# Five pairs of up products in seven half-sized products instead of three, with one load for two of their steps, and the low parts of unaltered weights formed by a DMA

## The chip, the cores and the metric

The kernel runs on one core of one Trainium2 chip. The metric is the device time of one execution in microseconds (us); lower is better. The engines are named as in the profile: PE (matrix products; its weight loads are PEld), DVE (vector), ACT (scalar functions), POOL, and SP, which here only issues DMAs.

## The reference

One decoder layer on a sequence of 512 tokens with 1024 features: forgetting attention, a layer norm, a gated MLP with a causal convolution of width 3, a second layer norm, and a gated embedding at the end. The change touches only the MLP:

```python
def conv_ffn(x, w_up, conv_w, conv_b, w_down):
    u, g = jnp.split(x @ w_up, [FFN_DIM], axis=-1)      # 1024 -> 2 x 2816
    g = causal_dwconv(g, conv_w, conv_b)
    return (jax.nn.gelu(g, approximate=False) * u) @ w_down
```

All inputs and outputs are float32.

## The kernel before

**Products.** PE takes operands in a shorter float format (`F32R`). Each operand is cut into a high part and a low part (what the high part leaves), and a product is three matmuls: high by high, high by low, low by high (`three`, L137). The activations are cut once; the weights are cut as they stream in.

**The stream of weights.** The class `Weights` (L57) holds one list of units of at most 128 x 1024 elements (512 KB) in the order of use. A unit is loaded by SP into a `raw` buffer (`load_to`, L74; four buffers of the tag `raw`, and every fifth unit of the MLP goes into a fifth place that `W.more` names, L259). It is then cut (`cut_to`, L95): ACT copies the raw weights into `whi`, which rounds them (L113), and DVE subtracts `whi` from them into `wlo` (L119). There are five `whi` and five `wlo` buffers (`SPLIT_BUFS`). Where a unit has a `make` function, DVE first forms sums or differences of weight blocks, one unit ahead of the cut. `get(i, 4)` (L125) cuts up to unit i+4 before PE's work on unit i is written down, so the cut of unit i+4 can begin when PE has finished unit i-1. There is a third way to make a low part, `by_dma` (L114): ACT writes minus the high part, and POOL issues a DMA that adds the weights to it from memory. No unit of this kernel asks for it.

**The MLP.** The 2816 hidden features are 22 blocks of 128, numbered f, and eleven pairs of blocks, numbered j. Parts 0 to 2 of the loop (L794) have three pairs each, part 3 has two. A *plain* pair is four up products (gate and up for two blocks) of 24 matmuls with 512 columns each. A *halved* pair (`UP_PAIRS`: 4, 7 and 9) takes the 2 x 2 blocks of x by weights in seven half-sized products instead of eight, in four steps, each for the gate (s=0) and for the up half (s=1), in `up_step` (L681):

- step 0 uses unaltered weights of block f0 (two products of 12 matmuls with 256 columns). Then ACT copies one half of the bank aside and zeroes it there (L706, L707), and DVE adds the two halves into the tile E (L709);
- step 1 uses t1 and t2, differences of weight blocks that `t12` (L188) forms with two DVE subtractions from the raw unit and a 256 KB side load;
- step 2 uses a third difference, `t3` (L202), formed from a second load of the same weights; DVE adds the result to E (L718);
- step 3 uses a fourth, `t4` (L208), with one product.

After the last step of a halved pair come its two convolutions and products (`conv_product`, L724) and then `operands` (L733), which makes the sums and the high and low parts that the down product wants. A plain pair has its first block's convolution and product in between, and so only the second block's product and `operands` at its end.

The down product of part p is also a seven-product form (`down`, L749). It runs in twelve steps of part p+1, in the calls of `between`: three steps of unaltered weights (`ua`), three `ub` (t12), three `uc` (t3) and three `ud` (t4). After the last step of each kind, `give` (L773) has DVE add finished banks to y (L555, L557), two adds of 512 columns for each; the banks x, y and z of the next kind are opened only then. Each pair of parts 1 and 2 has four down steps between its own: pair 3 has `ua` x3 and `ub`, pair 4 has `ub` x2 and `uc` x2, pair 5 has `uc` and `ud` x3, and pairs 6, 7 and 8 the same again.

**Order.** From block 2 on, DVE and ACT run in the order of the text (`manual_schedule`, L806). PE, SP and POOL are ordered by the tile framework's planner. A halved pair holds its two banks (one for gate, one for up) from step 0 to step 3.

Of the kernel before, what the change touches and what calls it, by code (L numbers as in the profile page):

```python
# [9 lines left out]
F32 = mybir.dt.float32  # L10
# [6 lines left out]
P = 128  # L17
# [7 lines left out]
KD = D // P  # L25
# [5 lines left out]

CHUNKS = (None, (1,) * 12, (1,) * 12, (2, 1) * 4)

UP_PAIRS = (4, 7, 9)
HALF = S // 2
ALPHA = 2.0 ** 0.25
EPS = 1e-5
# [2 lines left out]
UNIT = 1024  # L40
# [5 lines left out]
RAW_BUFS = 4  # L46
# [10 lines left out]
class Weights:  # L57
# [3 lines left out]
    def __init__(self, tc, pool):  # L61
        self.tc, self.nc, self.pool = tc, tc.nc, pool
        self.units, self.raw, self.parts = [], {}, {}
        self.loaded = self.cut = 0
        self.more, self.pieces = {}, {}

    def add(self, src, n=UNIT, inner=None, make=None, home=None, by_dma=False):

# [2 lines left out]
        self.units.append((src, n, inner, make, home, by_dma))  # L71
        return len(self.units) - 1

    def load_to(self, i):  # L74
        while self.loaded < min(i, len(self.units)):
            src, n, inner, make, _, _ = self.units[self.loaded]
            if self.loaded in self.more:
                t = self.more[self.loaded]()
            else:
                t = self.pool.tile([P, UNIT], F32, tag="raw", name=f"raw{self.loaded}", bufs=RAW_BUFS)  # L80
            v = t[:, :n]
            if inner is not None:
                v = v.rearrange("p (a b) -> p a b", b=inner)
            self.nc.sync.dma_start(v, src)
            if make is not None:
                make(None)
            self.raw[self.loaded] = t
            self.loaded += 1

    def make(self, i):  # L90
        if i < len(self.units) and i not in self.pieces and self.units[i][3] is not None:
            self.load_to(i + 1)
            self.pieces[i] = self.units[i][3](self.raw[i])

    def cut_to(self, i):  # L95
        while self.cut < min(i, len(self.units)):
            self.load_to(self.cut + 1)

            self.make(self.cut)
            self.make(self.cut + 1)  # L100
            src, n, inner, make, home, by_dma = self.units[self.cut]
            t = self.raw.pop(self.cut)
            behind = ExitStack()
            if home is not None:
                hi, lo, first = home()
                behind.enter_context(self.tc.issue_after(first))
            else:
                hi, lo = [self.pool.tile([P, UNIT], F32R, tag=g, name=f"{g}{self.cut}", bufs=SPLIT_BUFS)
                          for g in ("whi", "wlo")]
            c = 0  # L110
            for piece in [t[:, :n]] if make is None else self.pieces.pop(self.cut):
                e = c + piece.shape[-1]
                self.nc.scalar.activation(hi[:, c:e], piece, AF.Copy)  # L113
                if by_dma:  # L114
                    self.nc.scalar.activation(lo[:, c:e], piece, AF.Copy, scale=-1.0)
                    self.nc.gpsimd.dma_start(lo[:, c:e].rearrange("p (a b) -> p a b", b=inner), src,
                                             accum_op=ALU.add)
                else:
                    self.nc.vector.tensor_sub(lo[:, c:e], piece, hi[:, c:e].bitcast(F32))  # L119
                c = e  # L120
            behind.close()
            self.parts[self.cut] = (hi, lo)
            self.cut += 1

    def get(self, i, ahead=1):  # L125
        self.cut_to(i + 1 + ahead)
        more = any(u in self.more for u in range(self.cut, self.cut + RAW_BUFS))
        self.load_to(self.cut + RAW_BUFS - (not more))
        return self.parts[i]


# [1 line left out]
def trunk_layer(ctx: ExitStack, tc: tile.TileContext, xT, x2d, pT, wqk, wv0, wv1, wv2, bf, wo, wup, cwb,  # L133
                wdn, wpl, wg, bg, gm, bm, gf, bff, out):
    nc = tc.nc
# [18 lines left out]
    def half_rows(w, k0, n, cols):  # L154
        return w[k0 * P:(k0 + n) * P, cols * 512:(cols + 1) * 512].rearrange("(k p) c -> p k c", p=P)

    W = Weights(tc, base)
# [23 lines left out]
    aside = []  # L181

    def side(i):


        return aside[0][:, i, :]

    def t12(b11, i):  # L188
        def make(t):
            if t is None:  # L190
                to = side(i)
                if len(b11.shape) == 3:
                    to = to.rearrange("p (a b) -> p a b", b=P)
                nc.sync.dma_start(to, b11)
                return None
            t1, t2 = t[:, :512], side(i)
            nc.vector.tensor_sub(t1, t1, t2)
            nc.vector.tensor_sub(t2, t[:, 512:], t1)
            return [t1, t2]
        return make  # L200
# [7 lines left out]
    def t4(i):  # L208
        def make(t):
            if t is None:  # L210
                return None
            nc.vector.tensor_sub(t[:, :512], t[:, :512], side(i))
            return [t[:, :512]]
        return make

    def down_units(part):
        def b_rows(j, k0, n, cols):
            return half_rows(wdn, 2 * j + k0, n, cols)

        js = PAIRS[part]  # L220
        return [(b_rows(j, 0, 2, 0), UNIT, None) for j in js] + \
            [(b_rows(j, 0, 2, 1), UNIT, t12(wdn[2 * j * P:(2 * j + 1) * P, 0:512], i))
             for i, j in enumerate(js)] + \
            [(b_rows(j, 0, 2, 1), UNIT, t3) for j in js] + \
            [(b_rows(j, 1, 1, 0), 512, t4(i)) for i, j in enumerate(js)]

    def up_units(j):

        f0, f1 = 2 * j, 2 * j + 1

        def unit(f, q, make=None, k0=0):
            return W.add(wup[f, 1 - q][:, k0:], n=(KD - k0) * P, inner=P, make=make)

        return (lambda q: unit(f0, q), lambda q: unit(f1, q, t12(wup[f0, 1 - q][:, :4], 3 + q)),
                lambda q: unit(f1, q, t3), lambda q: unit(f0, q, t4(3 + q), 4))

    u_up, u_dn = {}, [[] for _ in PAIRS]
    for part in range(4):
        fs = range(6 * part, min(6 * part + 6, NF))
        todo = down_units(part - 1) if part else []  # L240

        for i in range(2 * len(fs)):
            f, q = fs[i // 2], i % 2
            j, n = f // 2, i % 4
            if j in UP_PAIRS:
                stages = up_units(j)
                for st, sq in (((0, 0),), ((0, 1),), ((1, 0), (1, 1)), ((2, 0), (2, 1)))[n]:
                    u_up[j, st, sq] = stages[st](sq)
            else:
                u_up[f, q] = W.add(wup[f, 1 - q], inner=P)  # L250
            for _ in range(CHUNKS[part][i] if part else 0):
                if todo:
                    src, c, make = todo.pop(0)
                    u_dn[part - 1].append(W.add(src, n=c, inner=512, make=make))
            if j in UP_PAIRS and n == 3:
                for sq in range(2):
                    u_up[j, 3, sq] = stages[3](sq)
        assert not todo
    for u in range(u_up[0, 1] + 5, len(W.units), 5):  # L259
        W.more[u] = lambda: aside[0][:, 5:7, :].rearrange("p a b -> p (a b)")  # L260
    u_r = [[W.add(half_rows(wdn, k, 2, n), inner=512) for k in REST[::2]] for n in range(2)]
    extra, last_cut = [], []

# [333 lines left out]
    def cut_tiles(kind, n, bufs, name, dtype=F32R, pool=spool):  # L597
        return [pool.tile([P, n, HALF], dtype, tag=f"{kind}{g}", name=f"{name}{g}", bufs=bufs) for g in "hl"]

    xt, sums = {}, []  # L600
    for t in range(NT):
        a, b = cut_tiles("S", 4, 4, f"x1t{t}", F32)
# [10 lines left out]
    for t in range(NT):  # L613
        ps = bank(f"ap{t}")
        tk = slice(t * P, (t + 1) * P)
        for k in range(KD):
            hi, lo = W.get(u_o[1][k // 2])
            c = slice(k % 2 * 512, k % 2 * 512 + 512)
# [175 lines left out]
    for part in range(4):  # L794
# [3 lines left out]
        def between():  # L798
            for _ in range(next(slots, 0)):
                next(before)  # L800

        for f in range(6 * part, min(6 * part + 6, NF)):
            q, j = f % 2, f // 2
# [6 lines left out]
            if f == 0:  # L810
                a, b = slice(0, HALF), slice(HALF, S)
# [8 lines left out]
                continue  # L820
            if j in UP_PAIRS:
                if q == 0:
# [23 lines left out]
            if q:  # L846
# [4 lines left out]
                else:  # L851
# [4 lines left out]
                    ops.append((h, l))  # L856
            if j not in UP_PAIRS:
                between()
# [9 lines left out]
    for i, t in enumerate(tiles):  # L868
        tk = slice(t * P, (t + 1) * P)
        for n in range(2):  # L870
            ps = bank(f"r{t}_{n}", "six")
            for k in range(len(REST)):
                hi, lo = W.get(u_r[n][k // 2])
                c = slice(k % 2 * 512, k % 2 * 512 + 512)
# [113 lines left out]
```

## Time and profile before

| | |
|---|---|
| median of 3 runs | 657.2 us (656.56 to 657.2) |
| the profiled execution | 656.48 us, its span 654.7 us |
| PE busy | 648.3 us, 99% |
| PEld busy | 561.7 us, 86% |
| DVE busy | 516.5 us, 79% |
| ACT busy | 339.6 us, 52% |
| POOL busy | 84.2 us, 13% |
| DMA: moved, share of 16 engines | 83.29 MB, 38.2% on the one data queue |
| granted clock | 0.999 |

"Busy" is the time in which an engine works on an instruction; "span" runs from the first to the last instruction. In the timeline a row has the start in us, the duration in us, the engine, the line of the kernel, the operation, output<-input by tile names, the shapes, the count, and in brackets the idle time before it and what ended that. Two instructions of the same kind in a row are merged and counted. Matmul rows overlap: their rate is read from the distance of their starts. In the MLP, g is the gate bank, u the up bank, x, y and z are banks of the down product.

### The profile page before, as it was taken

The numbers are of one execution on the slowest core, as the hardware profiler recorded it, in microseconds if no ns is written. First come the engines' busy times: TensorE is split into PE (matmuls) and PEld (weight loads), VectorE is DVE, ScalarE is ACT, GpSimd is POOL, SyncE is SP. The second block draws the span as 40 slices with busy tenths as digits, with TensorE's granted clock in tenths as the row PEclk, the third lists the DMA queues.
The fourth block names the chain that finished last, engine by engine and source line by source line (L and its number), as shares of the span: only waits on it lengthen the run. The fifth ranks groups of instructions, "written<-read, shape, count | busy, mean of one in ns | idle before, by whom it ended". The sixth has DMA issues, their size and how long they took to land.

```text
span 654.7 us, 9310 instructions
## 1 busy us (share of the span) xinstructions
PE 648.3 (99%) x3450; PEld 561.7 (86%) x3450; DVE 516.5 (79%) x830; ACT 339.6 (52%) x589; POOL 84.2 (13%) x78
## 2 busy tenths in 40 slices
PE   8999999999999999999999999999999999999997
PEld 7899888888888889888889988889988998888886
DVE  7674789988896599945769787879797998599464
ACT  6644777777775235734436454436445545425231
POOL 0000554445336020000000000000000000011000
PEclk9999999999999999999999999999999999999999
DMA  8533111122155313333334646434745463451321
GB/s 288 166 131 129 65 67 58 44 65 66 47 216 174 100 38 124 110 117 96 103 123 129 212 129 206 162 97 132 255 126 163 141 224 132 162 193 35 134 80 49
DMA packets 35485, 83.29 MB, mean 127 GB/s; under 512 B 3248, under 2 KB 7088, under 8 KB 35440
## 3 DMA queue, kind: packets, MB, share of 16 engines
q1 hardware_dynamic: 35440, 82.70, 38.2%
q8 instruction: 27, 0.44, 0.3%
q14 instruction: 18, 0.15, 0.1%
HBM read 80.46 MB, written 2.10 MB: 126 GB/s over the span
## 4 chain that ended last, share of the span: by engine, by line
PE 93%; DVE 3%; ACT 2%; issue 1%; DMA 1%; SPq 0%; DVEq 0%; ACTq 0%
PE u L142 16%; PE g L142 16%; PE pp L142 13%; PE x L142 7%; PE gt L142 7%; PE pv L142 7%; PE ao L142 3%; PE r L142 3%; PE z L142 3%; PE ap L142 3%; PE o L462 3%; PE t L449 3%; PE y L142 2%; PE pl L142 2%; PE s L418 2%; PE s L420 1%
## 5 line engine op out<-in xcount | busy, mean ns | idle before, releaser
L113 ACT ACTIVATE whi<-raw 128x1024 fp32r<-128x1024 f32 (+4 forms) x125 | 116.4, 936 | 97.2 <-PE u L142 17.1
L119 DVE TENSOR_TENSOR wlo<-raw,whi 128x1024 fp32r<-128x1024 f32 (+4 forms) x125 | 132.6, 1069 | 27.1 <-ACT whi L113 26.2
L436 POOL TENSOR_SCALAR pr<-pr,rl 128x128 f32<-128x128 f32 (+1 forms) x64 | 71.9, 1140 | 135.5 <-DVE rl L432 133.2
L142 PE MATMUL g<-x1h,whi 128*128 128x512 f32 (+1 forms) x180 | 63.0, 350 | 0.0
L142 PE MATMUL g<-x1l,whi 128*128 128x512 f32 (+1 forms) x180 | 62.9, 349 | 0.0
L142 PE MATMUL g<-x1h,wlo 128*128 128x512 f32 (+1 forms) x180 | 62.9, 349 | 0.0
L142 PE MATMUL u<-x1h,wlo 128*128 128x512 f32 (+1 forms) x172 | 61.5, 357 | 0.0
L142 PE MATMUL u<-x1l,whi 128*128 128x512 f32 (+1 forms) x172 | 61.5, 357 | 0.0
L142 PE MATMUL u<-x1h,whi 128*128 128x512 f32 (+1 forms) x172 | 61.4, 357 | 0.0
L568 POOL TENSOR_TENSOR mv<-mv,neghalf 128x1 f32<-128x1 f32 x8 | 11.6, 1445 | 379.1 <-DVE mv L567 356.8
L142 PE MATMUL pp<-xh,wlo 128*128 128x512 f32 x128 | 50.5, 395 | 0.0
L142 PE MATMUL pp<-xl,whi 128*128 128x512 f32 x128 | 50.0, 391 | 0.0
L142 PE MATMUL pp<-xh,whi 128*128 128x512 f32 x128 | 50.0, 391 | 0.0
L428 ACT ACTIVATE pr<-s,nm 128x128 f32<-128x128 f32 (+1 forms) x64 | 33.4, 524 | 17.4 <-DVE nm L427 15.3
L142 PEld LDWEIGHTS g<-x1h,whi 128*128 128x128 f32 x180 | 34.1, 189 | 4.5
L142 PEld LDWEIGHTS g<-x1l,whi 128*128 128x128 f32 x180 | 34.1, 189 | 4.5
L142 PEld LDWEIGHTS g<-x1h,wlo 128*128 128x128 f32 x180 | 34.1, 189 | 4.4
L142 PEld LDWEIGHTS u<-x1h,whi 128*128 128x128 f32 x172 | 32.5, 189 | 4.8
L142 PEld LDWEIGHTS u<-x1l,whi 128*128 128x128 f32 x172 | 32.5, 189 | 4.7
L142 PEld LDWEIGHTS u<-x1h,wlo 128*128 128x128 f32 x172 | 32.5, 189 | 4.7
L649 DVE SCALAR_TENSOR_TENSOR a<-g,cw,a 128x511 f32<-128x511 f32 x16 | 12.0, 748 | 24.8 <-ACT a L648 24.8
L142 PE MATMUL pv<-whi,xh 128*128 128x384 f32 (+1 forms) x96 | 30.1, 326 | 1.0 <-ACT whi L113 1.0
(539 smaller groups left out, 1660.8 us busy)
## 6 DMA issues: line engine op xcount, KB each, us to landing
raw<-wup SPq DMA_DIRECT2D x42, 512.0 KB
raw<-wdn SPq DMA_DIRECT2D x24, 512.0 KB
raw<-wqk SPq DMA_DIRECT2D x16, 512.0 KB
raw<-wo SPq DMA_DIRECT2D x8, 512.0 KB
side<-wup SPq DMA_DIRECT2D x8, 512.0 KB
raw<-wg SPq DMA_DIRECT2D x8, 512.0 KB
side<-wdn SPq DMA_DIRECT2D x7, 512.0 KB
raw<-wv SPq DMA_DIRECT2D x8, 384.0 KB
```

Source lines behind the costliest of these rows:

```text
L113: self.nc.scalar.activation(hi[:, c:e], piece, AF.Copy)
L119: self.nc.vector.tensor_sub(lo[:, c:e], piece, hi[:, c:e].bitcast(F32))
L142: nc.tensor.matmul(ps, lhsT, rhs, start=start and n == 0, stop=stop and n == 2, skip_group_check=on)
L418: nc.tensor.matmul(ps[:, :n], QA[:, q], KA[:, :n], start=True, stop=False)
L420: nc.tensor.matmul(ps[:, :n], qb[0:68, q], kb[0:68, :n], start=False, stop=True)
L428: nc.scalar.activation(pr[:, off:off + w], ps[:, :w], AF.Exp, bias=nm[:, i:i + 1], accum_out=ls[:, i:i + 1])
L436: nc.gpsimd.tensor_scalar_mul(pr[:, off:off + w], pr[:, off:off + w], rl[:, i:i + 1])
L449: nc.tensor.transpose(ps[:, w:w + P], pr[:, o:o + P], ident)
L462: nc.tensor.matmul(ps[:, q0:], V[:, j, h], p[:, o:o + w], start=j == 0 and n == 0, stop=j == NT - 1 and n == 1)
L568: nc.gpsimd.tensor_tensor(mv[:, 3:4], mv[:, 2:3], neghalf, op=ALU.pow)
L649: nc.vector.scalar_tensor_tensor(a[:, 1:], pg[:, :S - 1], cw[:, f, 1:2], a[:, 1:], op0=ALU.mult, op1=ALU.add)
```

## The change

- `UP_PAIRS` goes from (4, 7, 9) to (3, 4, 6, 7, 9): pairs 3 and 6 become halved, each directly before another halved pair.
- Step 2 of a halved pair has no load of its own. `Weights.again` adds a unit that uses the raw buffer of step 1's unit; for that, `t12` writes t1 over the side load instead of over the raw weights, and t2 into a second side place. The fifth raw place (`W.more`) is dropped, since the side tile now holds t2 there. The depth of loading ahead changes with it: `cut + 3`, plus one for each unit among the next four that needs no load.
- Units without a `make` in step 0 of the halved pairs and in the down product (`ua`) are marked `by_dma`: 10 and 9 units of 512 KB.

```diff
-UP_PAIRS = (4, 7, 9)
+UP_PAIRS = (3, 4, 6, 7, 9)
...
+    def again(self, i, make):
+
+        self.twice[len(self.units)] = i
+        return self.add(None, UNIT, make=make)
...
-            if self.loaded in self.more:
-                t = self.more[self.loaded]()
-            else:
-                t = self.pool.tile([P, UNIT], F32, tag="raw", name=f"raw{self.loaded}", bufs=RAW_BUFS)
+            if self.loaded in self.twice:
+                self.raw[self.loaded] = self.raw[self.twice[self.loaded]]
+                self.loaded += 1
+                continue
+            t = self.pool.tile([P, UNIT], F32, tag="raw", name=f"raw{self.loaded}", bufs=RAW_BUFS)
...
-            t = self.raw.pop(self.cut)
+            t = self.raw[self.cut]
...
-        more = any(u in self.more for u in range(self.cut, self.cut + RAW_BUFS))
-        self.load_to(self.cut + RAW_BUFS - (not more))
+        again = sum(u in self.twice for u in range(self.cut, self.cut + RAW_BUFS))
+        self.load_to(self.cut + RAW_BUFS - 1 + again)
...
-    def t12(b11, i):
+    def t12(b11, i, apart=None):
...
-            t1, t2 = t[:, :512], side(i)
-            nc.vector.tensor_sub(t1, t1, t2)
+            b11_ = side(i)
+            t1, t2 = (t[:, :512], b11_) if apart is None else (b11_, side(apart))
+            nc.vector.tensor_sub(t1, t[:, :512], b11_)
             nc.vector.tensor_sub(t2, t[:, 512:], t1)
...
-            return W.add(wup[f, 1 - q][:, k0:], n=(KD - k0) * P, inner=P, make=make)
-
-        return (lambda q: unit(f0, q), lambda q: unit(f1, q, t12(wup[f0, 1 - q][:, :4], 3 + q)),
-                lambda q: unit(f1, q, t3), lambda q: unit(f0, q, t4(3 + q), 4))
+            return W.add(wup[f, 1 - q][:, k0:], n=(KD - k0) * P, inner=P, make=make, by_dma=make is None)
+
+        return (lambda q: unit(f0, q), lambda q: unit(f1, q, t12(wup[f0, 1 - q][:, :4], 3 + q, 5 + q)),
+                lambda q: W.again(u_up[j, 1, q], t3), lambda q: unit(f0, q, t4(5 + q), 4))
...
-                    u_dn[part - 1].append(W.add(src, n=c, inner=512, make=make))
+                    u_dn[part - 1].append(W.add(src, n=c, inner=512, make=make, by_dma=make is None))
...
-    for u in range(u_up[0, 1] + 5, len(W.units), 5):
-        W.more[u] = lambda: aside[0][:, 5:7, :].rearrange("p a b -> p (a b)")
```

More of the change, by code (lines that the diff above doesn't have):

```diff
@@ L64, in __init__ @@
         self.loaded = self.cut = 0
-        self.more, self.pieces = {}, {}
+        self.twice, self.pieces = {}, {}
     def add(self, src, n=UNIT, inner=None, make=None, home=None, by_dma=False):
```

## The prediction

> **What bounds the kernel now.** I read the page first, then the busy time by windows, one window for each pair of the MLP.
>
> ```profile
> span 654.7 us, 9310 instructions
> ...
> PE 648.3 (99%) x3450; PEld 561.7 (86%) x3450; DVE 516.5 (79%) x830; ACT 339.6 (52%) x589; POOL 84.2 (13%) x78
> ...
> PE 93%; DVE 3%; ACT 2%; issue 1%; DMA 1%; SPq 0%; DVEq 0%; ACTq 0%
> ```
>
> ```profile
> core 0: us, PE busy (x) PEld busy (x) DVE busy (x) ACT busy (x) POOL busy (x), PEclk, DMA share, GB/s
> ...
> 313.94:346.58 32.64, 32.64 (x145) 27.03 (x144) 24.70 (x38) 12.87 (x19) 0.00 (x0) 1.00 0.36 119
> 346.58:377.69 31.11, 31.11 (x217) 29.15 (x216) 27.27 (x39) 16.71 (x26) 0.00 (x0) 1.00 0.53 183
> ...
> 499.48:536.03 36.55, 36.55 (x241) 33.66 (x240) 35.91 (x56) 20.05 (x32) 0.00 (x0) 1.00 0.51 170
> ```
>
> The page says: PE is the bound and the chain is PE's own work. The windows are pair 3 (plain), pair 4 (halved) and pair 9 (halved). PE never pauses in them, at full granted clock (1.00). So any PE work taken away is time taken away, as long as PE does not start to wait. But DVE is close behind, 27.27 of 31.11 us in pair 4. What matters is whether DVE, which works in the order of the text, is ever late.
>
> **Term 1, PE work removed.** Pairs 3 and 4 have the same four down steps, so their windows differ only by the form of the up product: 32.64 - 31.11 = 1.53 us. Pairs 3 and 6 change form: 2 x 1.53 = 3.06 us less. That is measured on whole pairs, so it holds what the narrow matmuls of the halved form lose.
>
> **Term 2, DVE's total.** A plain pair asks DVE for four low parts of 1024 columns. A halved one after the change asks, for gate and up each, four differences and three low parts of 512, one low part of 1024, one add of 256 and one of 512. With 1.23, 0.69 and 0.42 us from the rows below: 2 x (7 x 0.69 + 1.23 + 0.42 + 0.69) = 14.3 against 4.9, so 9.4 more for a pair, 18.8 for two. The DMA takes over the low parts of 9 `ua` units and of the 6 step-0 units of pairs 4, 7 and 9: 15 x 1.23 = 18.4 less. The total stays; it is where the work falls that changes. Pair 9 gets relief where DVE is fullest (35.91 of 36.55 us), but PE does not wait there, so that is worth nothing. ACT writes 19 more copies of 1.06 us and some small ones, and is half idle: no cost except in one place, below.
>
> **Term 3, the seam between two halved pairs (3 to 4, and 6 to 7).** This is new: before, a halved pair always followed a plain one. Here is PE in pair 4 and at its end, and DVE at both seams:
>
> ```profile
> start us, us, engine line op out<-in xcount [idle before <-releaser]
> ...
> 346.58 0.28 PE L142 MATMUL g<-x1h,whi 128*128 128x256 f32 x1
> ...
> 349.45 0.40 PE L142 MATMUL z<-whi,s1h 128*128 128x512 f32 x1
> ...
> 352.20 0.28 PE L142 MATMUL u<-x1h,whi 128*128 128x256 f32 x1
> ...
> 363.57 0.40 PE L142 MATMUL x<-whi,s0h 128*128 128x512 f32 x1
> ...
> 374.82 0.28 PE L142 MATMUL g<-x1h,whi 128*128 128x256 f32 x1
> ...
> 377.69 0.40 PE L142 MATMUL g<-x1h,whi 128*128 128x512 f32 x1
> ```
>
> ```profile
> 347.63 1.23 DVE L747 TENSOR_TENSOR s3l<-E,s3h 128x1024 fp32r<-128x1024 f32 x1 [0.19 <-ACT s3h L746]
> 348.77 0.68 DVE L197 TENSOR_TENSOR raw<-raw,side 128x512 f32<-128x512 f32 x1
> ...
> 351.30 0.69 DVE L197 TENSOR_TENSOR raw<-raw,side 128x512 f32<-128x512 f32 x1
> ...
> 353.84 0.42 DVE L709 TENSOR_TENSOR E<-g,side 128x256 f32<-128x256 f32 x1
> ...
> 357.71 0.42 DVE L709 TENSOR_TENSOR E<-u,side 128x256 f32<-128x256 f32 x1
> ...
> 359.78 1.29 DVE L555 SCALAR_TENSOR_TENSOR y<-y,x 128x512 f32<-128x512 f32 x2
> ...
> 379.01 0.75 DVE L649 SCALAR_TENSOR_TENSOR a<-E,cw,a 128x511 f32<-128x511 f32 x1 [0.93 <-ACT a L648]
> ...
> 386.17 1.23 DVE L747 TENSOR_TENSOR s4l<-E,s4h 128x1024 fp32r<-128x1024 f32 x1 [0.19 <-ACT s4h L746]
> 387.31 0.68 DVE L212 TENSOR_TENSOR raw<-raw,side 128x512 f32<-128x512 f32 x1
> ```
>
> PE's steps last 2.87 us (346.58 to 349.45, step 0), 2.75 us (to 352.20, a down step) and 1.44 us (two of step 3 from 374.82 to 377.69); those of a plain pair (32.64 - 4 x 2.75) / 4 = 5.4 us.
>
> Pair 4 now follows plain pair 3. DVE is done with pair 3's operands at 348.77, 2.2 us after PE has begun pair 4. From there DVE runs without a pause through two cuts with their differences, the add L709 for the gate, two more cuts, the add for the up half, one more cut, and the adds of x into y, the first done at 359.78 + 0.69 = 360.47. PE wants bank x (the first `uc` step) at 363.57, 17.0 us after the pair's start, so there are 3.1 us to spare.
>
> After a halved pair this cover is gone, because its convolutions, products and operands all come after its last step. PE leaves pair 4 at T = 377.69 and DVE is through the operands at 387.31, T + 9.6. If the next pair is halved too, DVE then has the same list to do, less one cut: `between` comes before step 3 in a halved pair, so the cut at 348.77 to 351.30 has been done by then. What is left:
> - to the end of the up half's add: 357.71 + 0.42 - 351.30 = 6.8 us, so T + 16.4. Step 1 of the up half writes the bank that this add reads, and takes 2.87 us: T + 19.3.
> - to the first add of x: 360.47 - 351.30 = 9.2 us, so T + 18.8.
>
> PE reaches the `uc` step at T + 17.0 if nothing holds it. So it is held 1.8 us by the banks of the down product, or 2.3 us if the whole up bank is guarded. Queued behind the late adds are the cuts for the steps that follow, so nothing is made up before; DVE catches up later in the pair, where its list is shorter than PE's. What stands ahead in ACT's queue at T adds some more:
>
> ```profile
> 374.84 1.06 ACT L113 ACTIVATE whi<-raw 128x1024 fp32r<-128x1024 f32 x1 [1.58 <-PE z L142]
> 376.45 0.38 ACT L722 ACTIVATE E<-g 128x256 f32<-128x256 f32 x1 [0.55 <-PE g L142]
> ...
> 378.18 1.51 ACT L648 ACTIVATE a<-E,cw 128x512 f32<-128x512 f32 x2
> ```
>
> The copy at 374.84 will be followed by one more of 1.06 us (the negative for the DMA), which fills the idle 0.55 us and pushes the copies of E and the convolution behind it by up to 0.5 us; I take 0.3. So a seam costs 1.8 to 2.8 us; I take 2.4, nearer to the guarded bank. That PE does wait on such adds is seen where the next pair is plain:
>
> ```profile
> 391.32 0.39 PE L142 MATMUL g<-x1h,whi 128*128 128x512 f32 x1
> 391.83 0.50 PE L142 MATMUL x<-whi,b0h 128*128 128x512 f32 x1
> ```
>
> ```profile
> 391.09 1.28 DVE L557 TENSOR_TENSOR y<-y,x 128x512 f32<-128x512 f32 x2
> ```
>
> x opens at 391.83, right after the first of the two adds (391.09 + 0.69); with matmuls 0.23 us apart PE lost some 0.3 us, twice as much work per step lying before it (pair 5 is plain). These small waits stay.
>
> **Term 4, low parts by DMA.** No row of before shows an adding DMA. Nearest are the loads of 512 KB:
>
> ```profile
> q1 hardware_dynamic: 35440, 82.70, 38.2%
> ```
>
> ```profile
> 7.57 0.34 SPq L84 DMA_DIRECT2D raw<-wqk  x1
> ```
>
> ```profile
> 13.58 1.06 ACT L113 ACTIVATE whi<-raw 128x1024 fp32r<-128x1024 f32 x1 [1.09 <-DMA raw<-wqk]
> ```
>
> 82.70 MB cost 38.2% of 654.7 us of all engines: 1.6 us for 512 KB at the least. In the crowded start such a load was used 6.0 us after its issue. An adding DMA also reads what it adds to, so from 1.6 us to twice 6.0 = 12 us; I take 6, the crowded load. The tightest place is again the seam, since pair 3's last steps are short and a unit is cut four steps ahead. The buffer for pair 4's gate comes free 2 x 1.44 + 2.75 + 2.87 = 8.5 us before T, and two copies of 1.06 us are done at T - 6.4. That of the up half comes free at T - 2.9, the copies are done at T - 0.8, and its step begins at T + 2.87 + 2.75 = T + 5.6; the low part is used by the third matmul, 0.2 us later. Since DVE holds the seam anyway, both may be some 1.8 us late: each has about 8.5 us. At 6 us the cost is nothing; beyond 8.5 every us costs one, at 12 us about 3 more a seam. In front of pairs 3, 6 and 9 lie plain steps of 5.4 us, so there it is covered twice over.
>
> A rule that speaks against this: the Trainium skill, page "SBUF — State Buffer", section "SBUF: two separate sides", says that a DMA issued from POOL has its descriptors written by POOL, which is locked out while DVE runs certain two-port operations. The same page excepts two-input operations such as this kernel's DVE rows; no run here shows it. By the rule without the exception the sum would be that of the late low parts below.
>
> The fifth raw place is lost: the load for unit i+7 now goes out when unit i+3 is cut, three steps (8.2 us or more) before use, against 6.0 us for a crowded load. Cost nothing; SP's loads wait for buffers already. The dropped second loads (6 of 512 KB) gain nothing, since nobody waits on loads.
>
> **Sum.** Against the profiled execution: 656.48 - 3.06 + 2 x 2.4 = 658.2 us. The median of the runs shown, 657.2, lies 0.7 above that execution, so I predict 658.9. With seams of 1.8 to 3.0 us: 657.7 to 660.1. A measurement can tell about 0.2%, 1.3 us, from no change.
>
> **Rivals.**
> - *The seam is covered*: 657.2 - 3.06 = 654.1 us. PE's order is the planner's, not the text's (it put one matmul of g ahead of x at 391.32). If it places work of the next steps ahead of the late banks, or DVE gets through its list 2 us sooner, PE keeps the whole saving. This decides if the up half's add is done by T + 14.0. Against it: every step after this waits for a cut that stands behind the same adds. Chance 0.20.
> - *Half a seam*: PE waits for 0.9 to 1.9 us at each, 656 to 658 us, no change to be measured. Chance 0.17.
> - *Late low parts*: the adding DMA takes 12 us, or waits for a pause of DVE. The pause that ends at 379.01 (T + 1.3) would be the first sure one; with 6 us on top the gate's low part comes at T + 7.3 instead of T + 0.2, 7.1 us late, 4.7 more than the seam costs already. 658.9 + 6 to 9.4 = 665 to 668 us. For it: nothing like it is in the trace. Chance 0.13.
>
> The forecast has the rest, 0.50. The range for 8 in 10 goes from 653.5, below the covered seam, to 663, with part of the late low parts. Faster by over 0.2%: 0.21. Within: 0.25. Slower: 0.54, the late low parts and most of the forecast.
>
> **What would show it.** Right: pairs 4 and 7 in the changed profile take 33 to 34 us instead of 31.1, and pairs 3 and 6 take 31.1; PE's idle time lies in the first 20 us of pairs 4 and 7, ended by DVE's add into E (L709 of before) or into y; DVE runs without a pause in that stretch. DVE's total is within 5 us of 516.5. Wrong: PE without idle time at the seam (the first rival), or PE waiting there for a DMA (the third), which would show in the waits with a DMA as releaser, and in pairs 3, 6 and 9 as well if the DMA is very slow.

## The result: 675.7 us, 3% slower

| | before | after |
|---|---|---|
| median of 4 runs each, us | 656.88 (656.37 to 657.2) | 675.69 (674.28 to 680.78) |
| ratio to before, 95% interval | | 1.0301 (1.0246 to 1.0356) |
| span of the profiled execution, us | 654.7 | 673.3 |
| granted clock | 0.999 | 0.992 |

The direction was forecast, the size was not: 658.9 us was predicted, 663 was the end of the range.

On the page of after PE is idle for 21.6 us of the span, against 6.4 before. It is no less busy (651.7 us against 648.3), in part because what it does at half clock (below) counts longer. The chain that gave PE 93% before now has 9% DVE, 8% issue and 7% DMA. POOL has a queue of its own now.

```profile
span 673.3 us, 9750 instructions
...
PE 651.7 (97%) x3594; PEld 569.5 (85%) x3594; DVE 517.0 (77%) x847; ACT 369.7 (55%) x640; POOL 104.2 (15%) x97
...
q1 hardware_dynamic: 35728, 81.65, 37.6%
q0 software_dynamic: 3888, 9.96, 8.6%
...
PE 72%; DVE 9%; issue 8%; DMA 7%; ACT 2%; POOL 0%; SPq 0%; POOLq 0%; DVEq 0%; ACTq 0%
```

Busy time by windows of after; the rows are pairs 3, 4, 6, 7 and 9:

```profile
core 0: us, PE busy (x) PEld busy (x) DVE busy (x) ACT busy (x) POOL busy (x), PEclk, DMA share, GB/s
314.13:345.24 31.11, 31.11 (x218) 29.15 (x216) 26.27 (x42) 19.18 (x32) 2.58 (x3) 1.00 0.73 179
345.24:378.99 33.75, 31.88 (x219) 29.31 (x218) 30.35 (x47) 19.08 (x31) 0.36 (x1) 1.00 0.54 157
408.31:444.25 35.94, 32.09 (x217) 29.09 (x216) 27.93 (x46) 20.94 (x34) 4.72 (x5) 1.00 0.84 213
444.25:478.93 34.68, 32.85 (x219) 30.71 (x218) 30.57 (x46) 19.33 (x32) 0.39 (x1) 0.95 0.53 153
508.03:554.58 46.55, 38.65 (x242) 34.71 (x240) 34.23 (x54) 21.46 (x34) 3.34 (x3) 0.93 0.65 167
```

An undisturbed halved pair takes 31.11 us, and pair 3 does. Pair 4 loses 2.64 us, pair 7 3.57, pair 6 4.83, and pair 9 takes 46.55 against 36.55 us before: 10.00 more. That is 21.0 us lost; less the 3.06 us of PE work saved, 18.0 of the 18.6 us between the two spans. Of the rest, 0.3 us is in pair 5 and 0.2 us ahead of pair 3. So the two pairs behind a seam lost 6.2 us, of 4.8 predicted, while pairs 6 and 9, where nothing was predicted, lost 14.8.

What ends PE's pauses in pairs 6 and 9 is the adding DMA. The timeline of PE in after, rows with idle time in front (the first is of pair 4, the fifth of pair 7):

```profile
347.02 0.39 PE L148 MATMUL g<-x1h,wlo 128*128 128x256 f32 x1 [1.38 <-DMA wlo<-wup]
...
409.61 0.39 PE L148 MATMUL g<-x1h,wlo 128*128 128x256 f32 x1 [0.90 <-DMA wlo<-wup]
413.90 0.47 PE L148 MATMUL x<-wlo,a3h 128*128 128x512 f32 x1 [0.94 <-ACT whi L119]
...
422.01 0.47 PE L148 MATMUL x<-wlo,a4h 128*128 128x512 f32 x1 [1.76 <-DMA wlo<-wdn]
...
446.48 0.39 PE L148 MATMUL g<-x1h,wlo 128*128 128x256 f32 x1 [1.83 <-DMA wlo<-wup]
...
512.82 0.47 PE L148 MATMUL x<-wlo,a6h 128*128 128x512 f32 x1 [1.29 <-DMA wlo<-wdn]
522.41 0.77 PE L148 MATMUL x<-wlo,a7h 128*128 128x512 f32 x1 [6.61 <-DMA wlo<-wdn]
```

All of these matmuls read a `wlo` that a DMA adds to. That of 413.90 is put down to ACT, but its tile's DMA landed at 413.76.

Three things make those DMAs late. All show in the timelines of POOL (in brackets, its idle time) and of ACT in after (L121 is the negative copy, L752 one of the operands of the pair before), and in the line on landings under the instructions of L122:

```profile
398.77 0.86 POOL L122 DMA_DIRECT2D wlo<-wup  x1 [53.17 <-ACT wlo L121]
403.46 1.22 POOL L122 DMA_DIRECT2D wlo<-wdn  x1 [3.83 <-ACT wlo L121]
...
503.18 1.20 POOL L122 DMA_DIRECT2D wlo<-wdn  x1 [3.86 <-ACT wlo L121]
513.00 1.20 POOL L122 DMA_DIRECT2D wlo<-wdn  x1 [8.62 <-DVE y L563]
513.73 1.39 POOL L122 DMA_DIRECT2D wlo<-wup  x1
522.61 1.22 POOL L122 DMA_DIRECT2D wlo<-wdn  x1 [7.49 <-issue]
```

```profile
503.59 1.05 ACT L121 ACTIVATE wlo<-raw 128x1024 fp32r<-128x1024 f32 x1
509.25 1.06 ACT L752 ACTIVATE s8h<-E 128x1024 fp32r<-128x1024 f32 x1 [0.65 <-DVE E L749]
511.17 1.04 ACT L121 ACTIVATE wlo<-raw 128x1024 fp32r<-128x1024 f32 x1
513.06 1.04 ACT L121 ACTIVATE wlo<-raw 128x1024 fp32r<-128x1024 f32 x1
```

```profile
DMA to landing us min/median/max: 6.2/8.1/11.1
```

1. *The landing is slow.* The last line is for the 19 DMAs of L122 in after, from POOL's start. Those of 398.77 and 403.46 started right behind their copies and landed 10.8 and 10.3 us later, behind the matmuls' need at 408.5 and 412.8.
2. *POOL holds issues back.* The copy of 503.59 was done at 504.64, but its DMA began at 513.00, 8.36 us later; in a free stretch it is 0.31 to 0.44. What it waited for is not what the brackets name: the DMA of 503.18 landed at 512.68. In the same way 522.61 falls 0.3 us behind the landing that PE waited for until 522.41. Six of the 19 waited for a landing, or in line behind an issue that did, for 1.5 to 8.5 us. PE wanted the low part of 513.00 at 515.6 and had it at 522.4.
3. *Copies come late.* ACT makes the copies of 511.17 and 513.06 only behind the operands of pair 8 (509.25), since it works in the order of the text. What this costs by itself is measured below (e8, e9).

On top of the long pause comes the clock. Busy time by windows of after: behind the pause of pair 7 (444.5 to 446.5), and around that of pair 9 (515.6 to 522.4):

```profile
447.40:449.00 1.60, 1.60 (x10) 1.60 (x9) 1.56 (x3) 0.78 (x2) 0.00 (x0) 0.50 0.99 219
...
518.99:525.82 6.83, 3.41 (x8) 2.77 (x9) 2.70 (x5) 0.00 (x0) 1.22 (x1) 0.50 0.87 157
```

PE works 3.4 us at half clock after each (447.31 to 450.72 and 522.41 to 525.82 by the trace's record of the clock), and so loses 1.7 us twice.

### The profile page after: what moved, and what is told of

Its sections match the earlier page's. It is cut to its first block, busy times and chain, and to the rows that moved or that the text cites. A ratio compares the mean times of both kernels' runs of the same rounds, so it can differ in the third digit from the quotient of the medians.

```text
span 673.3 us, 9750 instructions
## 1 busy us (share of the span) xinstructions
PE 651.7 (97%) x3594; PEld 569.5 (85%) x3594; DVE 517.0 (77%) x847; ACT 369.7 (55%) x640; POOL 104.2 (15%) x97
## 3 DMA queue, kind: packets, MB, share of 16 engines
q0 software_dynamic: 3888, 9.96, 8.6%
## 4 chain that ended last, share of the span: by engine, by line
PE 72%; DVE 9%; issue 8%; DMA 7%; ACT 2%; POOL 0%; SPq 0%; POOLq 0%; DVEq 0%; ACTq 0%
PE pp L148 13%; PE g L148 10%; PE u L148 9%; PE gt L148 7%; PE pv L148 6%; PE x L148 4%; PE r L148 3%; PE ao L148 3%; PE ap L148 3%; DVE wlo L125 3%; PE o L468 3%; DMA wlo<-wdn 3%; PE t L455 2%; DMA raw<-wdn 2%; PE z L148 2%
## 5 line engine op out<-in xcount | busy, mean ns | idle before, releaser
L119 ACT ACTIVATE whi<-raw 128x1024 fp32r<-128x1024 f32 (+4 forms) x141 | 131.4, 937 | 108.4 <-DVE raw L213 15.6
L125 DVE TENSOR_TENSOR wlo<-raw,whi 128x1024 fp32r<-128x1024 f32 (+5 forms) x122 | 127.0, 1048 | 32.9 <-ACT whi L119 32.0
L148 PE MATMUL g<-x1h,wlo 128*128 128x256 f32 (+1 forms) x172 | 58.3, 339 | 4.1 <-DMA wlo<-wup 4.1
L148 PE MATMUL g<-x1h,whi 128*128 128x256 f32 (+1 forms) x172 | 58.1, 338 | 0.0
L148 PE MATMUL g<-x1l,whi 128*128 128x256 f32 (+1 forms) x172 | 57.9, 337 | 0.0
L148 PE MATMUL u<-x1h,wlo 128*128 128x512 f32 (+1 forms) x164 | 56.0, 341 | 0.3 <-DMA wlo<-wup 0.2
L148 PE MATMUL u<-x1l,whi 128*128 128x512 f32 (+1 forms) x164 | 55.8, 340 | 0.0
L148 PE MATMUL u<-x1h,whi 128*128 128x512 f32 (+1 forms) x164 | 55.8, 340 | 0.0
L148 PE MATMUL pp<-xh,wlo 128*128 128x512 f32 x128 | 50.7, 396 | 0.0
L148 PE MATMUL pp<-xl,whi 128*128 128x512 f32 x128 | 50.0, 391 | 0.0
L148 PE MATMUL pp<-xh,whi 128*128 128x512 f32 x128 | 50.0, 391 | 0.0
L122 POOL DMA_DIRECT2D wlo<-wup x10 | 9.5, 954 | 201.1 <-ACT wlo L121 110.7
L148 PEld LDWEIGHTS g<-x1h,wlo 128*128 128x128 f32 x172 | 33.3, 194 | 7.9 <-DMA wlo<-wup 4.7
L148 PEld LDWEIGHTS g<-x1l,whi 128*128 128x128 f32 x172 | 33.3, 194 | 3.3
L148 PEld LDWEIGHTS g<-x1h,whi 128*128 128x128 f32 x172 | 33.3, 194 | 3.3
L148 PEld LDWEIGHTS u<-x1h,wlo 128*128 128x128 f32 x164 | 31.1, 190 | 4.1 <-issue 0.4
L148 PEld LDWEIGHTS u<-x1h,whi 128*128 128x128 f32 x164 | 31.1, 190 | 3.6
L148 PEld LDWEIGHTS u<-x1l,whi 128*128 128x128 f32 x164 | 31.1, 190 | 3.6
L148 PE MATMUL pv<-whi,xh 128*128 128x384 f32 (+1 forms) x96 | 30.5, 331 | 0.3 <-ACT whi L119 0.2
```

Of the source, the lines that this page charges most:

```text
L148: nc.tensor.matmul(ps, lhsT, rhs, start=start and n == 0, stop=stop and n == 2, skip_group_check=on)
```

## The experiments

Two theories stood against each other after the result. A: the adding DMA is what was not foreseen, by its landing, its place in ACT's order and POOL's waits for a ring of limited size. B: the seam is dearer than worked out, and the DMAs are late because everything is. All diffs are against the changed kernel, and all ratios against before.

**The adding DMA taken out, and alone.** Run e1 keeps the five halved pairs and gives all low parts back to DVE; e4 has the pairs of before and keeps only the shared load; e2 has the pairs of before with the DMA.

```diff
 e1, lines 240 and 262 (each line's beginning left out)
-    ... make=make, by_dma=make is None)
+    ... make=make, by_dma=False)
 e4: the same, and as e2:
-UP_PAIRS = (3, 4, 6, 7, 9)
+UP_PAIRS = (4, 7, 9)
```

> The change with every low part made by DVE again (five halved pairs, shared load, no adding DMA). Theory A, the adding DMA is what costs: its waits in PE (some 15 us) and the halved clock after the long ones go, and what is left is the two seams. DVE gets 23 us of work back, some of it right before the seams, so they cost 2.6 to 3.7 us each: 656.9 - 3.1 + 5.2 to 7.4 = 659 to 661 us. Theory B, the seams and DVE cost most: DVE gets more work, so 675 us or more. Theory C, the shared load with four raw buffers costs most: 670 us or more.

> The three old halved pairs and no adding DMA: of the change only the shared load of steps 1 and 2 and the loss of the fifth raw place are left. Theories A and B: nothing waits on loads, 656.9 within 0.7 us. Theory C (four raw buffers are too few): 660 us or more, with waits of DVE for loads in the halved pairs.

> The change with the three old halved pairs (4, 7, 9): shared load and adding DMA, no two halved pairs in a row. Theory A: pair 9 stands as in the changed kernel and loses its 10 us there, the rest a little: 665 to 669 us. Theory B (the seams): no seam is left, 656 to 658 us. Theory C (four raw buffers): 665 us or more, with PE waiting behind loads and not behind the adding DMA.

Measured: e1 661.96 us, ratio 1.0071 (1.0059 to 1.0083); e4 656.51, 0.9997 (0.9988 to 1.0005); e2 668.54, 1.0177 (1.0164 to 1.019). The DMA alone, without any seam, costs 1.8%; the pairs alone cost 0.7%; the shared load and the lost fifth raw place cost nothing with the pairs of before. That is A, though e1 lies 1 us above the range expected for it. In e2 PE's waits for the adding DMAs of `wdn` units have the same sum as in after, 9.7 us; from the waits of e2 (total, times, longest), where the profile puts two of POOL's waits down to a DMA:

```profile
POOL wlo L122 <- DMA wlo<-wdn: 18.0, 2, 9.3
...
PE x L148 <- DMA wlo<-wdn: 9.7, 3, 6.7
```

**POOL's ring.** e3 doubles the memory that the kernel reserves for the descriptors of POOL's DMAs (the ring).

```diff
-    nc = bacc.Bacc("TRN2", target_bir_lowering=False, num_devices=1, dynamic_dma_scratch_size=1024)
+    nc = bacc.Bacc("TRN2", target_bir_lowering=False, num_devices=1, dynamic_dma_scratch_size=2048)
```

> The change with twice the descriptor scratch for DMAs that POOL issues (2048 instead of 1024 bytes). Theory A1, POOL's queue is held because a third adding DMA, or a second one of the down weights, doesn't fit beside those in flight: the five waits of 1.5 to 8.5 us between ACT's copy and the issue go, the 6.8 us pause in pair 9 and the 1.9 us one in pair 6 with them, and the halved clock behind the long one: 663 to 667 us. The waits for landings of 7 to 11 us stay (pairs 4, 6 and 7). Theory A2, the transfers themselves are too slow because the 16 engines are full: more of them in flight land later, 672 us or more.

Measured: 670.16 us, 1.0208 (1.0191 to 1.0226). The waits are gone, as the timeline of POOL in e3 shows at the place of the 8.36 us, but the time lies between the two expectations:

```profile
503.36 1.20 POOL L122 DMA_DIRECT2D wlo<-wdn  x1 [3.86 <-ACT wlo L121]
505.16 1.20 POOL L122 DMA_DIRECT2D wlo<-wdn  x1 [0.60 <-ACT wlo L121]
512.80 0.88 POOL L122 DMA_DIRECT2D wlo<-wup  x1 [6.43 <-ACT wlo L121]
```

All 19 issues follow their copies within 0.30 to 0.46 us, with up to three under way. The landings have become slower in turn, 7.3, 8.9 and 11.8 us. So the larger ring is worth 0.9% of the 3.0. The queue's 3888 packets are 9 on each of 16 engines for a `wup` unit and 17 for a `wdn` unit (10 x 9 + 9 x 17 = 243, x 16); in after, 26 were under way together, and an issue that would have made them 34 or more waited. Where between these the limit of 1024 bytes lies is open.

**The adding itself.** e7 is e3 with a plain DMA in place of the adding one. It leaves out the adding: the low parts are whole weights.

```diff
-    self.nc.gpsimd.dma_start(lo[:, c:e].rearrange("p (a b) -> p a b", b=inner), src,
-                             accum_op=ALU.add)
+    self.nc.gpsimd.dma_start(lo[:, c:e].rearrange("p (a b) -> p a b", b=inner), src)
```

> As with the scratch of 2048 bytes, but the DMAs that POOL issues write the weights without adding them (the low parts are then whole weights, so the adding is left out). Theory A3, the adding is what makes them land after 7 to 12 us: they land after 3.3 to 6 us like SP's loads, PE no longer waits for them, the seams stay: 659 to 663 us. Rival, the way through POOL and the full engines is what is slow: they still land after 7 us or more, and the time stays at 667 to 671 us.

Measured: 663.18 us, 1.0098 (1.0084 to 1.0112), 0.2 us above the range of theory A3, and close to e1. The page and the issues of this line in e7:

```profile
q0 software_dynamic: 3888, 9.96, 4.6%
```

```profile
DMA to landing us min/median/max: 4.4/6.0/7.6
```

The same packets and bytes keep the engines busy for 4.6% of the span instead of 8.5% (e3), and land in 6.0 us instead of 8.9 (e3). That alone is 1.1% of time, about as much as the ring's 0.9%. At 6 us, the landing that the prediction took, the DMA costs 0.3% more than e1, hardly more than the intervals tell apart. It is not free: PE still waits 1.8 us for two landings (until 418.46 and 515.03), and DVE is spared 19 low parts that it makes in e1.

**The seam.** e6 is e1 with the low parts of the operands of pairs 3 and 6 set to zero by POOL; it leaves out these low parts (`operands` gets `j` for that). That takes some 2 us of DVE's work from each seam.

```diff
-            nc.vector.tensor_sub(l, src, h.bitcast(F32))
+            if j in (3, 6):
+                nc.gpsimd.memset(l.bitcast(F32), 0.0)
+            else:
+                nc.vector.tensor_sub(l, src, h.bitcast(F32))
```

> The change without the adding DMA, and in pairs 3 and 6 the low parts of the down product's operands are left out (POOL writes zeros instead): DVE has 2.1 us less to do at each seam, and nothing else moves. Theory A, the seam is DVE's list after the last step: each seam gets 2.1 us shorter, 662.0 - 4.1 = 657.9, between 657 and 659 us. Rival, the seam is the chain of copies and activations on ACT, or PE's order: 661 to 662.5 us.

Measured: 657.32 us, 1.0005 (0.9996 to 1.0014), 4.6 us below e1. Pairs 4 and 7 by windows of e1, then of e6:

```profile
346.42:380.61 34.19, 31.64 (x219) 29.13 (x218) 30.81 (x48) 18.92 (x31) 0.00 (x0) 1.00 0.39 126
441.09:475.93 34.84, 31.86 (x218) 29.17 (x217) 30.95 (x47) 18.80 (x31) 0.00 (x0) 1.00 0.42 126
```

```profile
345.29:377.52 32.23, 31.49 (x218) 29.12 (x217) 28.78 (x45) 18.76 (x32) 0.00 (x0) 1.00 0.45 134
437.91:470.88 32.97, 31.87 (x219) 29.18 (x218) 29.04 (x45) 18.61 (x31) 0.00 (x0) 1.00 0.41 137
```

The seams shrink from 3.1 and 3.7 us over 31.11 to 1.1 and 1.9, by 2.0 and 1.9 us: what DVE is spared (30.81 to 28.78, 30.95 to 29.04), PE has. A further 1.1 us lies ahead of pair 4 (346.42 against 345.29), where the edit has done nothing yet. This is the seam as predicted, DVE's list. That it is longer than predicted in e1 only because DVE has the DMA's cuts back is not shown: in e7, where the DMA takes them, the same pairs lose 2.7 and 3.9 us (below).

**The pairs apart.** e5 halves pairs 3, 5, 7 and 9, without the DMA: one pair more than before, and no seam.

```diff
-UP_PAIRS = (3, 4, 6, 7, 9)
+UP_PAIRS = (3, 5, 7, 9)
 lines 240 and 262 as in e1
```

> Four halved pairs, 3, 5, 7 and 9, none behind another, low parts all by DVE, shared load. Theory A, a halved pair costs only where it follows a halved one: one pair more than before gains its 1.53 us, 656.9 - 1.5 = 655.4, between 654.7 and 656.2 us. Rival: each further halved pair overloads DVE (9.4 us more for a pair) wherever it stands: 657 us or more.

Measured: 655.3 us, 0.9983 (0.9974 to 0.9992), the gain of one halved pair (1.53 us) in full. Its chain is PE's own work again, on the page of e5:

```profile
PE 95%; DVE 2%; ACT 1%; issue 1%; DMA 1%; SPq 0%; DVEq 0%; ACTq 0%
```

This version is faster than both kernels, than before by 0.2%.

**The DMA in that version.** e8 gives e5 the DMA for its eight step-0 units only, where the lead looked longest.

```diff
-UP_PAIRS = (3, 4, 6, 7, 9)
+UP_PAIRS = (3, 5, 7, 9)
 line 262 (its beginning left out)
-    ... make=make, by_dma=make is None))
+    ... make=make))
```

> Four halved pairs apart (3, 5, 7, 9), with the adding DMA for the step-0 units only (8 of 512 KB) and DVE for the down product. Theory A, the adding DMA costs only where its lead is shorter than its landing of about 8 to 10 us: behind a plain pair the lead is longer, so within 0.7 us of the same pairs without it, about 655.4 us. Rival, any adding DMA costs, by crowding the loads and by PE's waits: 657 us or more.

Measured: 661.95 us, 1.0079 (1.0065 to 1.0093): theory A missed. Seven of the eight cost 0.2 us or less; the up half of pair 9 cost the rest. ACT, POOL and PE in e8:

```profile
499.55 1.06 ACT L752 ACTIVATE s8h<-E 128x1024 fp32r<-128x1024 f32 x1 [0.65 <-DVE E L749]
501.46 1.05 ACT L121 ACTIVATE wlo<-raw 128x1024 fp32r<-128x1024 f32 x1
```

```profile
502.93 0.89 POOL L122 DMA_DIRECT2D wlo<-wup  x1 [13.32 <-ACT wlo L121]
```

```profile
510.45 0.55 PE L148 MATMUL u<-x1h,wlo 128*128 128x256 f32 x1 [3.16 <-ACT whi L119]
```

The copy stands behind pair 8's operands, the DMA starts 0.4 us after it and lands 7.4 us later, at 510.31; PE was there at 506.9. The bracket of PE's row names ACT, but the matmul reads the low part, and it starts 0.14 us behind that landing. The clock is halved for 6.83 us from 509.42 on, and the step loses 5.5 us in all. The ring is not at work here, since no other adding DMA is under way, and 7.4 us is the shortest landing of the eight (up to 9.9). What is left is ACT's order. e9 tests that, in the kernel of e8, by cutting this unit ahead of those operands:

```diff
+                if f == 17:
+                    W.cut_to(W.cut + 1)
```

> The four pairs apart with the adding DMA for step 0, and in block 17 (the last of plain pair 8) one more unit is cut before the block's product and operands are written down, so that ACT makes the copies of the late unit (step 0, up half, of pair 9) some 8 us sooner. Theory A, that DMA was late because ACT's copies stood behind the operands in the order of the text: the 3 us pause and the halved clock behind it go, 655.4 to 656.5 us. Rival, the landing in the crowded stretch is what is late: it lands late from any start, 660 us or more.

Measured: 656.38 us, 0.9993 (0.9984 to 1.0002). The copy of this unit stands at 497.85 now, ahead of the operands, the DMA starts 3.6 us earlier (499.31), and the matmul comes 0.5 us late instead of 3.3, from the timeline of PE in e9:

```profile
507.33 0.36 PE L148 MATMUL u<-x1h,wlo 128*128 128x256 f32 x1 [0.33 <-ACT whi L119]
```

So ACT's order was the cause there. The DMA still gains nothing over e5 (655.3 us).

**One pair more.** e10 halves pairs 1, 3, 5, 7 and 9, without the DMA.

> Five halved pairs 1, 3, 5, 7 and 9, none behind another, no adding DMA. Pair 1 follows a plain pair, but also the sums of x that every halved pair reads: DVE has the last product (0.7), eight adds of 512 (5.5), four low parts of 1024 (4.9), pair 0's operands (3.9) and a cut (2.5 us) to do before the add that frees the gate's bank, some 17 us after pair 1 begins, and PE is there after 5.7. Theory A, it is DVE's list that decides and not what kind of pair stands ahead: PE waits about 11 us there and runs at half the clock behind it, 664 to 669 us. Rival, only a halved pair behind a halved one costs: 656.9 - 3.1 = 653.8 us.

Measured: 660.98 us, 1.0063 (1.005 to 1.0076), slower as theory A had it, but by less. Pair 1 comes where DVE has no time to spare, in the windows of e10:

```profile
262.00:283.00 21.00, 16.09 (x109) 14.93 (x108) 21.00 (x32) 14.11 (x21) 0.00 (x0) 0.94 0.14 43
```

DVE is busy for all 21.00 us, and PE waits 4.91 us for the add into E. I had expected a wait of 11 us, having counted DVE work in this stretch that was done earlier: the eight adds of the sums run from 257.69 to 265.04, and pair 1 begins at 271.03.

## Why the prediction was wrong

**Term 1 (3.06 us of PE work) was right.** Pair 3 takes 31.11 us, and e5 gains its 1.6 us with one halved pair more.

**Term 2 (DVE's total stays) was right:** 517.0 us against 516.5.

**Term 3 (the seam) was right in mechanism and too small in size.** The rows of DVE in after:

```profile
355.01 0.68 DVE L205 TENSOR_TENSOR side<-raw,side 128x512 f32<-128x512 f32 x1
...
361.42 0.42 DVE L715 TENSOR_TENSOR E<-u,side 128x256 f32<-128x256 f32 x1
...
363.49 1.28 DVE L561 SCALAR_TENSOR_TENSOR y<-y,x 128x512 f32<-128x512 f32 x2
```

and of PE:

```profile
361.89 0.39 PE L148 MATMUL u<-xsh,whi 128*128 128x256 f32 x1 [0.46 <-DVE E L715]
...
364.87 0.40 PE L148 MATMUL x<-whi,s0h 128*128 128x512 f32 x1
```

PE begins pair 4 at T = 345.24. DVE is through the operands at T + 9.8 (predicted 9.6), through the up half's add at T + 16.6 (16.4), and the first add of x is done at T + 18.9 (18.8). The guarded bank decides, as taken: PE's step 1 of the up half starts 0.05 us after that add, and the `uc` step at T + 19.6 (19.3). Pair 4 lost 2.64 us for 2.4. But 1.4 us of that lie at its first use of a low part (L148, at 347.02), which the page puts down to the adding DMA. Run e7, whose DMAs land in 6 us, shows the seam without that wait; pairs 4 and 7 by windows of e7, and PE's waits for the adds into E in both together:

```profile
345.48:379.30 33.82, 31.89 (x219) 29.18 (x218) 30.51 (x47) 19.09 (x32) 0.00 (x0) 1.00 0.45 144
440.70:475.75 35.05, 31.90 (x218) 29.19 (x217) 31.35 (x48) 19.08 (x31) 0.01 (x1) 1.00 0.44 139
```

```profile
PE g L147 <- DVE E L714: 3.5, 2, 2.4
PE u L147 <- DVE E L714: 1.5, 2, 0.7
```

Pair 4 loses 2.71 us there, so by this comparison the wait for the DMA cost nothing on top in after: the same time is lost at the adds otherwise. The first of these waits is at the gate's bank, which the prediction left out. By its own rows the gate's add is done at T + 9.6 + 353.84 + 0.42 - 351.30 = T + 12.6, and PE wants that bank after two steps and two down steps, at T + 11.2. The sum does not change by it, since the up half's add comes later.

Pair 7 is not the forecast seam in after: PE waits 1.83 us for the adding DMA, loses 1.7 us at half clock behind it, and has no wait for DVE left. In e7 it loses 3.94 us. There DVE stood still for 2.44 us, until 440.94, for a load into a raw buffer, and so was through the operands only at T + 11.1; the prediction put waits for loads at nothing, and whether the lost fifth raw place is behind this one is open. The seams of e7 thus take 6.65 us where the sum has 4.8: the term was too small by 1.9 us.

**Term 4 (low parts by DMA cost nothing) is the step that failed**, and of it four parts:
- "I take 6, the crowded load". The landing took 6.2 us at the least, 8.1 in the median, 11.1 at the most. The bounds, 1.6 to 12, held it; the value chosen was that of a load that adds nothing, and e7 measures 6.0 for just that.
- "In front of pairs 3, 6 and 9 lie plain steps of 5.4 us, so there it is covered twice over". Before pair 3 this held. Before pairs 6 and 9 it did not: 14.8 of the 21.0 us are lost there. Two DMAs for the first steps of pair 6 had a lead of some 9.5 us and landed 10.8 and 10.3 us after their start. For the later units of a pair the lead was reckoned from when a buffer comes free; it is set by when ACT, in the order of the text, gets to the copies, behind the operands of the pair before (e8, e9).
- "Each has about 8.5 us" held in pair 4, where the gate's low part landed 7.74 us after its issue. In pair 7 it landed 8.18 us after its issue and 8.55 us after its copy was done; that PE's pause ahead of the seam could halve the clock was not in the prediction.
- POOL's issue was taken to follow the copy. Two DMAs of a `wdn` unit at a time did not fit into the ring, and one waited up to 8.5 us for the landing of the other; with the larger ring (e3) none does.

Against 658.9 us the run took 16.8 more, by the medians: 5.5 by the small ring (after to e3), 7.0 by the adding (e3 to e7), and 4.3 that are left in e7, whose seams and waits for landings are named above. The ratios divide the whole loss in the same way: the pairs with their seams 0.7% above before (e1), the DMA from POOL as such 0.3% on top (e7), its adding 1.1% (e3), the small ring 0.9% (after). That the change was slower at all was no luck: it is slower by 1.0% even with the landing that was assumed (e7).

The third rival, PE waiting for a DMA, was nearest. Its first form, a landing of 12 us, was near the far end of what was measured (11.1), but it was priced at the seams alone, and 14.8 of the 21.0 us fell elsewhere. Its other form, that POOL waits for a pause of DVE, is refuted by e3: all 19 issues began 0.30 to 0.46 us after their copies, and through four of them (323.29, 344.71, 413.72 and 512.80) DVE worked with no pause over 0.04 us. The Trainium skill, page "SBUF — State Buffer", section "SBUF: two separate sides", has two-input operations take that lock only against a POOL operation that reads SBUF; these issues, which ran beside such operations, agree with it. The first rival, the covered seam, is refuted by e1; without a seam (e5) its gain is real.

## What to carry to other kernels

Work handed to a DMA is not free because the total of an engine stays the same: it buys a latency, and the lead for it runs from the moment when the engine ahead of the issue comes to it in its own order, not from when a buffer is free. Price an operation that no trace shows at the far bound until one run measures it, and ask how many of its kind may be under way at once. A form that saves work on the bounding engine but bunches the work of the next one goes where it has the lighter form as neighbours and the next engine has time to spare: four halved pairs apart were 0.2% faster than before (e5), five with two seams 0.7% slower (e1), and five apart, with the first where DVE is full, 0.6% slower (e10).

## What the runs showed of the hardware

- An adding DMA of 512 KB costs the DMA engines almost twice a plain one (8.5% of the span in e3 against 4.6% in e7, for the same 9.96 MB) and lands in 8.9 instead of 6.0 us in the median, both with the larger ring. Over all runs the adding ones took 6.0 to 11.8 us.
- An issue from POOL that found no place in the ring waited, and the profile of after names other events as its releaser (at 513.00 DVE, though the landing was at 512.68); the waits were recognised by a landing 0.3 us ahead.
- A short pause can halve PE's clock. The Trainium skill, page "TensorE: Matmul & The Clock Gate", section "Why this matters for your kernels", warns of gaps of more than about 3 us. Here the idle time of 1.83 us that ended at 446.48 in after was followed by 3.4 us at half clock, while one of 2.10 us in e1, in the same pair, was not (the pair's window has 1.00). The timeline of PE in e1:

```profile
454.61 0.39 PE L148 MATMUL g<-xsh,whi 128*128 128x256 f32 x1 [2.10 <-DVE E L715]
```

  With the pauses of over 3 us (pair 9 in after, e8, e10) came 6.83 us at half clock, twice as long, and they began inside the pause. The clock's record gives a hint at what decides for the short ones. The half-clock stretches of one run start whole multiples of 3.413 us apart: at 447.31 and 518.99 in after (21 times), at 349.02 and 666.46 in e3 (93 times). Laid out in such steps, the pause of 1.83 us in after and one of 1.88 us in e3 (until 347.53), both followed by half clock, lie inside one step, while that of 2.10 us in e1 lies across the end of one. But in e2 1.85 us of a pause (until 507.13) lie inside one step without half clock behind it, so the limit itself is not shown.
- In two crowded stretches of after, POOL's DMA sent its first packet 4.7 to 4.8 us after POOL's start (398.77, 498.44), against 2.0 to 2.9 us in the others that found no such DMA under way. Why is open.
